# Moving all loads of a normalisation kernel to one DMA queue, with a 2 KB write ahead of the stores

## The chip, the cores and the metric

The kernel runs on one core of a Trainium2 chip. The metric is the device time of one execution in microseconds (us). Before the change it was 626.81 us, the median of 3 runs (626.70 to 626.87).

## The reference

Each of 4 x 8 x 16 = 512 channels of 256 x 256 float32 values is normalised to mean 0 and variance 1 and multiplied by its gamma:

```python
mu = x.mean(axis=(3, 4), keepdims=True)
var = ((x - mu) ** 2).mean(axis=(3, 4), keepdims=True)
out = (x - mu) / np.sqrt(var + 1e-5) * gamma[None, :, :, None, None]
```

134.2 MB are read and 134.2 MB are written, and each value takes few operations.

## The kernel before

The data is cut into 32 units of 128 rows x 8192 floats (4 MB; a row is 32 KB). Six slots in on-chip memory hold units. A unit is loaded, summed on VectorE (DVE), its squares are summed on ScalarE (ACT), a small matmul combines the rows of a channel, VectorE scales the slot in place, and the slot is stored. When the store has landed, the slot takes the load of the unit six further on. Loads are issued from SyncE's queue (SP), stores from ScalarE's. Only the first loads are dealt over both queues. The parts (`# ...` marks cuts):

```python
    def load(u, queue):
        queue.dma_start(out=slots[u % AHEAD][:], in_=xv[u])

    g_row = singles.tile([1, G * C], F32, name="g_row")
    for u in range(AHEAD):                       # AHEAD = 6
        if u == 1:
            nc.scalar.dma_start(out=g_row[:], in_=gv[None, :])
        load(u, nc.scalar if u in (1, 3) else nc.sync)
    # ...
    nc.vector.tensor_copy(out=g_rep[:], in_=g_row[:]...)          # gamma, before all units
    # ... 8 small matmuls spread gamma over the partitions
    nc.vector.tensor_copy(out=g_col[:], in_=g_ps[:])

    for u in range(U):                           # U = 32
        t = slots[u % AHEAD]
        nc.vector.reduce_sum(out=st[:, u, 0:1], in_=t[:], axis=AX.X)
        square = nc.scalar.activation(out=junk[:], in_=t[:], func=ACTF.Square, accum_out=st[:, u, 1:2])
        # ... matmul, variance, root, reciprocal, scale
        nc.vector.tensor_scalar(out=t[:], in0=t[:], scalar1=ps[:, 0:1],
                                scalar2=scale[:, u : u + 1], op0=ALU.add, op1=ALU.mult)
        nc.scalar.dma_start(out=ov[u], in_=t[:])
        if u + AHEAD < U:
            load(u + AHEAD, nc.sync)
```

## Time and profile before

| what | value | from |
|---|---|---|
| time, median of 3 | 626.81 us | runs |
| span in the profile | 625.2 us | page |
| DVE busy / ACT busy | 71% / 38% | page |
| share of the two DMA queues, of 16 engines' span | 52.8% + 46.8% | page |
| DMA rate | 429 GB/s mean, 436 in most slices | page |
| one 32 KB packet on one DMA engine | 1.213 us | packet records |
| 512 such packets one after another | 621.1 us (619.0 at the measured spacing) | product |
| from the start of one packet to the next on one engine | 1.209 us (the records overlap by 0.004) | packet records, median |

The next lines are from the profile page: the span, the mean busy share of the 16 DMA engines in 40 slices of 15.6 us (tenths), the GB/s moved in each slice, and the two queues with packets, MB and share of 16 engines' span. q1 is SyncE's queue, q10 ScalarE's.

```profile
span 625.2 us, 626 instructions
...
DMA  8999999999999999999999999999999999999998
GB/s 369 436 417 424 434 436 436 436 436 437 434 436 434 426 426 430 434 436 436 436 434 434 436 434 434 430 426 430 434 436 436 436 432 434 436 436 434 426 426 365
...
q10 hardware_dynamic: 4898, 142.61, 52.8%
q1 hardware_dynamic: 4320, 125.83, 46.8%
```

The two shares add to 99.6%: the DMA engines hardly ever rest. The slowest slices are the first and last, and the third and fourth, in which the first store begins; the others lie at 426 to 437.

The start of the timeline (start us, duration us, what; in brackets the idle time before it and what ended it):

```profile
0.80 1.90 SPq L48 DMA_DIRECT2D xt<-in_x_dram  x4
0.80 0.53 ACTq L54 DMA_DIRECT2D g_row<-in_gamma_dram  x1
...
1.37 0.84 ACTq L48 DMA_DIRECT2D xt<-in_x_dram  x2
...
2.06 0.68 DVE L79 COPY g_rep<-g_row 1x1024 f32<-1x1024 f32 x1 [2.06 <-DMA g_row<-in_gamma_dram]
...
20.32 8.69 DVE L103 TENSOR_REDUCE st<-xt 128x1 f32<-128x8192 f32 x1 [13.70 <-DMA xt<-in_x_dram]
...
35.38 0.35 ACTq L130 DMA_DIRECT2D out_dram<-xt  x1
```

gamma is there at 2.06 us, the first unit only at 20.32 (loads 0 and 1 share the engines), and the first store is issued at 35.38.

The waits view (who waited for what: us in total, times, longest), the time from issue to landing (KB each, median us), and the page's chain of work that ended last, by engine:

```profile
ACT junk L104 <- DMA xt<-in_x_dram: 229.0, 24, 16.6
DVE st L103 <- DMA xt<-in_x_dram: 111.2, 24, 13.7
```

```profile
out_dram<-xt ACTq DMA_DIRECT2D x32, 4096.0 KB, 67.1
xt<-in_x_dram SPq DMA_DIRECT2D x30, 4096.0 KB, 33.8
```

```profile
another core or an unknown queue 64%; DMA 16%; DVE 13%; SPq 1%; PE 1%; issue 0%; ACT 0%
```

Both compute engines wait for loads. A store takes 67 us to land though its own transfer is 8 packets on each engine, 9.7 us, so about seven such transfers (its own, other stores and the loads between them) pass meanwhile.

**Packet records.** The trace lists every DMA packet with start, duration, size and queue, but without its engine. I assigned each packet to the engine whose previous packet ended at that moment (within 12 ns). For the kernel before this gives 16 clean rows of 512 large packets. "Slow-packet time" below is the sum of what packets took above 1.213 us, divided by 16 engines. In the kernel before it is 0.71 us at the start, 0.62 us at about 43 us, where the first store's packets begin, and 0.08 us in all the time after 100 us.

### The profile page before, as it was taken

The page shows a single profiled execution, that of the slowest core. Times are in us where ns is not written, and L with a number is a line of the kernel's source. Part 1 is how long each engine was busy: PE and PEld are TensorE (multiplying, and loading weights), DVE is VectorE, ACT ScalarE, POOL GpSimd, SP SyncE. Part 2 cuts the span into 40 slices and gives each one's busy share as a digit, 9 for nine tenths or more (in the row PEclk, how much of TensorE's full clock was granted, in tenths as well). Part 3 has the DMA queues.
Part 4 walks back from the last instruction along what each step waited for, and adds up shares of the span by engine and source line. Part 5 has one row for each costly group of instructions (what it writes and reads, how often), then busy time and mean ns, then how long its engine had stood idle before and what let it go on. Part 6 is the DMA issues. An engine that isn't in the chain of part 4 may idle for free.

```text
span 625.2 us, 626 instructions
## 1 busy us (share of the span) xinstructions
PE 21.4 (3%) x80; PEld 19.5 (3%) x80; DVE 443.2 (71%) x162; ACT 238.8 (38%) x98; POOL 1.3 (0%) x9
## 2 busy tenths in 40 slices
PE   2000000000000000000000000000000000000000
PEld 2000000000000000000000000000000000000000
DVE  0699999998867668676687766776667867668620
ACT  0444444444444224443244432344423443224400
POOL 0000000000000000000000000000000000000000
DMA  8999999999999999999999999999999999999998
GB/s 369 436 417 424 434 436 436 436 436 437 434 436 434 426 426 430 434 436 436 436 434 434 436 434 434 430 426 430 434 436 436 436 432 434 436 436 434 426 426 365
DMA packets 9220, 268.46 MB, mean 429 GB/s; under 512 B 1025, under 2 KB 1026, under 8 KB 1026
## 3 DMA queue, kind: packets, MB, share of 16 engines
q10 hardware_dynamic: 4898, 142.61, 52.8%
q1 hardware_dynamic: 4320, 125.83, 46.8%
q14 instruction: 2, 0.02, 0.0%
HBM read 134.22 MB, written 134.22 MB: 429 GB/s over the span
## 4 chain that ended last, share of the span: by engine, by line
another core or an unknown queue 64%; DMA 16%; DVE 13%; SPq 1%; PE 1%; issue 0%; ACT 0%
DMA xt<-in_x_dram 9%; DVE st L103 8%; DMA out_dram<-xt 7%; DVE xt L126 4%; SPq L48 1%; PE ps L112 1%; ACT std L117 0%; DVE nvar L113 0%; DVE rstd L121 0%; DVE scale L123 0%
## 5 line engine op out<-in xcount | busy, mean ns | idle before, releaser
L103 DVE TENSOR_REDUCE st<-xt 128x1 f32<-128x8192 f32 x32 | 277.9, 8684 | 111.2 <-DMA xt<-in_x_dram 111.2
L104 ACT ACTIVATE junk<-xt 128x8192 uint8<-128x8192 f32 x32 | 225.0, 7030 | 272.2 <-DMA xt<-in_x_dram 229.0
L126 DVE TENSOR_SCALAR xt<-xt,ps,scale 128x8192 f32<-128x8192 f32 x32 | 145.6, 4550 | 1.2
L117 ACT ACTIVATE std<-nvar,eps_t 128x1 f32<-128x1 f32 x32 | 9.4, 294 | 79.6 <-DVE nvar L113 79.6
L112 PE MATMUL ps<-st,navg 128*128 128x2 f32 x64 | 17.9, 349 | 568.0 <-DVE st L103 568.0
L112 PEld LDWEIGHTS ps<-st,navg 128*128 128x128 f32 x64 | 16.0, 312 | 569.8 <-issue 569.8
L113 DVE TENSOR_SCALAR nvar<-ps 128x1 f32<-128x1 f32 x32 | 9.2, 287 | 23.8 <-PE ps L112 23.8
L121 DVE RECIPROCAL rstd<-std 128x1 f32<-128x1 f32 x32 | 5.3, 164 | 11.6 <-ACT std L117 11.6
L104 ACT ACTIVATION_READ_ACCUMULATOR junk<-xt 128x1 f32 x32 | 6.0, 186 | 0.0
L123 DVE TENSOR_TENSOR scale<-rstd,g_col 128x1 f32<-128x1 f32 x32 | 5.1, 159 | 1.1
L84 PE MATMUL g_ps<-one,g_rep 1*128 1x1 f32 x16 | 3.5, 346 | 2.9 <-DVE g_rep L79 2.9
L84 PEld LDWEIGHTS g_ps<-one,g_rep 1*128 1x128 f32 x16 | 3.5, 325 | 2.9 <-POOL navg L68 2.9
L90 DVE COPY g_col<-g_ps 128x8 f32<-128x8 f32 x1 | 0.2, 166 | 3.7 <-PE g_ps L84 3.7
L74 ACT ACT_TABLE_LOAD x1 | 1.3, 1283 | 2.2 <-issue 2.2
L79 DVE COPY g_rep<-g_row 1x1024 f32<-1x1024 f32 x1 | 0.7, 681 | 2.1 <-DMA g_row<-in_gamma_dram 2.1
L64 POOL TENSOR_SCALAR_AFFINE_SELECT navg<-navg 128x128 f32<-128x128 f32 x1 | 0.4, 403 | 0.1
L68 POOL TENSOR_SCALAR_AFFINE_SELECT navg<-navg 128x128 f32<-128x128 f32 x1 | 0.4, 398 | 0.1
L63 POOL MEMSET navg<- 128x128 f32 x1 | 0.2, 220 | 0.0
L74 ACT ACTIVATE root_eps<-eps_t 128x1 f32<-128x1 f32 x1 | 0.2, 203 | 0.0
L147 POOL MEMSET const-bfloat16-1.0<- 128x1 bf16 x1 | 0.1, 101 | 0.0
L147 POOL MEMSET const-uint8-127<- 128x1 uint8 x1 | 0.1, 101 | 0.0
L147 POOL MEMSET const-float32-0.0<- 128x1 f32 x1 | 0.1, 98 | 0.3 <-issue 0.3
(3 smaller groups left out, 0.3 us busy)
## 6 DMA issues: line engine op xcount, KB each, us to landing
out_dram<-xt ACTq DMA_DIRECT2D x32, 4096.0 KB, 67.1
xt<-in_x_dram SPq DMA_DIRECT2D x30, 4096.0 KB, 33.8
xt<-in_x_dram ACTq DMA_DIRECT2D x2, 4096.0 KB, 33.3
g_row<-in_gamma_dram ACTq DMA_DIRECT2D x1, 0.5 KB
```

The source lines that it names most:

```text
L48: queue.dma_start(out=slots[u % AHEAD][:], in_=xv[u])
L74: nc.scalar.activation(out=root_eps[:], in_=eps_t[:], func=ACTF.Sqrt)
L79: nc.vector.tensor_copy(out=g_rep[:], in_=g_row[:].rearrange("o (n k) -> o n k", n=NG).unsqueeze(3).to_broadcast([1, NG, K, S]),)
L84: nc.tensor.matmul(out=g_ps[:, n : n + 1], lhsT=g_rep[:, n].rearrange("o k s -> o (k s)"), rhs=one[:], start=True, stop=True,)
L103: nc.vector.reduce_sum(out=st[:, u, 0:1], in_=t[:], axis=AX.X)
L104: square = nc.scalar.activation(out=junk[:], in_=t[:], func=ACTF.Square, accum_out=st[:, u, 1:2],)
L112: nc.tensor.matmul(out=ps[:], lhsT=navg_w, rhs=st[:, u], start=True, stop=True)
L113: nc.vector.tensor_scalar(out=nvar[:, u : u + 1], in0=ps[:, 0:1], scalar1=ps[:, 0:1], scalar2=ps[:, 1:2], op0=ALU.mult, op1=ALU.add,)
L117: nc.scalar.activation(out=std[:, u : u + 1], in_=nvar[:, u : u + 1], func=ACTF.Sqrt, bias=eps_t[:], scale=-1.0,)
L121: nc.vector.reciprocal(out=rstd[:, u : u + 1], in_=std[:, u : u + 1])
L123: nc.vector.tensor_mul(out=scale[:, u : u + 1], in0=rstd[:, u : u + 1], in1=g_col[:, g : g + 1],)
L126: nc.vector.tensor_scalar(out=t[:], in0=t[:], scalar1=ps[:, 0:1], scalar2=scale[:, u : u + 1], op0=ALU.add, op1=ALU.mult,)
```

## The change

The intent can only be inferred: the loads become one plain stream, and a tiny early write to `out` may pay in advance what the first store pays. 32 rows of the first output unit get 64 bytes each, two rows per DMA engine, which the real store overwrites later.

```diff
-    def load(u, queue):
-        queue.dma_start(out=slots[u % AHEAD][:], in_=xv[u])
-
+    def load(u):
+        nc.sync.dma_start(out=slots[u % AHEAD][:], in_=xv[u])
 
     g_row = singles.tile([1, G * C], F32, name="g_row")
+
+    touch = singles.tile([P, 16], F32, name="touch")
+    nc.vector.memset(touch[:], 0.0)
     for u in range(AHEAD):
-        if u == 1:
+        load(u)
+        if u == 0:
+            nc.scalar.dma_start(out=ov[0, 0::4, 0:16], in_=touch[0::4])
             nc.scalar.dma_start(out=g_row[:], in_=gv[None, :])
-        load(u, nc.scalar if u in (1, 3) else nc.sync)
 ...
-            load(u + AHEAD, nc.sync)
+            load(u + AHEAD)
```

## The prediction

> **What bounds the kernel now.** The DMA engines, nearly without a pause. The page's third part puts the queues at 52.8% and 46.8% of 16 engines' span, 99.6% together; its second part shows about 436 GB/s in most slices and 429 on average. DVE is busy 71%, ACT 38%. In the trace's DMA packet records every one of the 8192 packets of 32 KB takes about 1.213 us, 512 follow each other on each of 16 engines, and hardly any gap is over 0.1 us: 512 x 1.213 = 621.1 us of a 625.2 us span. (The Trainium skill, "DMA: Bandwidth & Descriptors", section "Where 436 GB/s comes from", gives a ceiling of 435 GB/s; 16 x 32,768 B / 1.213 us = 432 agrees.) So only about 4 us is not pure transfer:
> - about 2.1 us before the first load packet moves, though the first load is issued at 0.80 (timeline);
> - the engines' first packet, 2.0 us instead of 1.2: about 0.9 us with its successors;
> - one bubble at 41 to 44 us, where ScalarE's queue turns from its last load to the first store: 22 packets take 1.3 to 1.9 us, together about 0.65 us per engine;
> - about 1.3 us after the last store packet.
>
> The waits view's long times (ACT for loads 229 us, DVE 111 us) are engines waiting for this traffic.
>
> **What the change does.**
> 1. Loads 1 and 3 move from ScalarE's queue to SP's. Bytes and packets stay. The same skill page, "Issuing engines are not separate DMA queues", says that both queues feed the same engines, so no bandwidth is lost or won; in this trace packets from one queue alone (the last 20 us, stores only) also take 1.213 us. Load 0 no longer shares with load 1: it lands near 11.9 us (estimate: 8 packets x 1.21 + 2.1) instead of 20.3, the first reduction starts there, and the first store is issued near 27 us instead of 35.4. That moves compute by 8 us, all hidden: six loads are 58 us of transfer, and the queues stay non-empty until the end.
> 2. The touch: 2048 bytes, 32 rows of 64 B, two per engine, behind a tiny DVE memset. Its presumable aim is to pay each engine's first-write cost during startup. If the 0.65 us bubble is a first-write cost, up to 0.65 us is saved; if it comes from a queue turning from loads to stores, part 1 already removes it, since ScalarE's queue then holds no large loads. The touch itself may add 0.1 to 0.5 us at the start (estimate: two tiny packets per engine, and the same bubble in the worst case).
>
> **On the critical path:** only the bubble and the start, under 1 us of 627. I expect about 0.4 us less.
>
> **Predicted: 626.4 us, range 625.6 to 627.3.** Chances: faster by over 2% 0.01, within 2% 0.98, slower by over 2% 0.01.
>
> **What would show it.** Steps 1: the first DVE reduction starts near 12 us, the first store's issue is near 27 us, queue bytes 134 MB on each, DMA rate 436 in the middle slices. Step 2: no packets over 1.3 us at the first store; slightly longer first packets. Wrong: the same bubble at about 28 us; a first slice clearly below 369 GB/s.
>
> **What would make it wrong.** A single queue with six loads could leave gaps between packets (slices under 430 before 28 us). The small writes to rows 128 KB apart could stall the engines for microseconds at the start. Another phase between loads and stores could change the packet time itself.

## The result, and the profile after

The changed kernel took 627.20 us (median of 4 runs, 627.09 to 627.40), before 626.84 us beside it (4 runs, 626.70 to 627.08). The ratio is 1.0006 with a 95% interval of 0.9988 to 1.0023: the same. (Ratios here are the mean time of one kernel's fast runs over that of the other's in the same rounds, so not quite the ratio of the quoted medians.) Executions over 1.5% slower than the fastest of the same kernel are left out of the means.

The page, for the lines shown of before:

```profile
span 625.4 us, 628 instructions
...
DMA  9999999999999999999999999999999999999998
GB/s 369 436 413 428 434 436 436 436 436 436 434 436 432 428 424 432 434 436 434 436 436 436 434 436 434 425 428 434 430 436 434 436 436 436 434 434 436 428 432 354
...
q1 hardware_dynamic: 4608, 134.22, 49.9%
q10 hardware_dynamic: 4658, 134.22, 49.7%
```

The two shares are 99.6% again; the bytes are now even. The first slice has the same 369 GB/s, so one queue feeds the engines as well as two did. The third slice has its dip again (413, it was 417).

The timeline:

```profile
0.98 0.58 ACTq L57 DMA_DIRECT2D out_dram<-touch  x1
...
1.60 0.67 ACTq L58 DMA_DIRECT2D g_row<-in_gamma_dram  x1
...
11.74 0.68 DVE L82 COPY g_rep<-g_row 1x1024 f32<-1x1024 f32 x1 [10.80 <-DMA g_row<-in_gamma_dram]
...
13.11 7.03 ACT L107 ACTIVATE junk<-xt 128x8192 uint8<-128x8192 f32 x1 [9.30 <-DMA xt<-in_x_dram]
16.15 0.17 DVE L93 COPY g_col<-g_ps 128x8 f32<-128x8 f32 x1 [3.73 <-PE g_ps L87]
16.23 8.67 DVE L106 TENSOR_REDUCE st<-xt 128x1 f32<-128x8192 f32 x1
...
31.28 0.39 ACTq L133 DMA_DIRECT2D out_dram<-xt  x1
```

Load 0 is there at 13.1 us, when ACT starts on it, 7 us earlier than before. But DVE starts only at 16.23. In DVE's program order the two copies for gamma stand before the first reduction, and gamma now arrives at 11.7 us instead of 2.06, because it is issued behind the touch on ScalarE's queue. In the packet records the touch's two 64-byte packets per engine start near 6.1 and 7.3 us, its completion packet near 8.6, gamma's 512 bytes at 10.1: one small packet per 1.2 us, each taking turns with a 32 KB load packet. The Trainium skill, "DMA: Bandwidth & Descriptors", section "Queues, rings and completion order", says that an engine goes round its queues packet by packet; this trace agrees from 6.1 us on, and shows what that costs a small transfer. The turns are not the whole delay: the touch was issued at 0.98 us, and three load packets pass on every engine before its first packet. In the kernel before, load 1 (issued at 1.37, first packet at 6.13) waits as long, and the first stores of the kernels with all loads on SyncE's queue start 3.5 to 4.9 us after their issue. The turn-taking alone does not explain this, and no run here does.

Waits, landing times and chain:

```profile
ACT junk L107 <- DMA xt<-in_x_dram: 251.2, 27, 10.1
DVE st L106 <- DMA xt<-in_x_dram: 111.2, 26, 5.1
```

```profile
xt<-in_x_dram SPq DMA_DIRECT2D x32, 4096.0 KB, 53.2
out_dram<-xt ACTq DMA_DIRECT2D x32, 4096.0 KB, 47.8
out_dram<-touch ACTq DMA_DIRECT2D x1, 2.0 KB, 8.5
```

```profile
DVE 71%; another core or an unknown queue 18%; PE 4%; DMA 2%; ACT 2%; issue 1%; ACTq 0%
```

Three things are to be seen. DVE waits for loads for exactly as long as before, 111.2 us. The landing times moved from 67.1 + 33.8 = 100.9 us to 47.8 + 53.2 = 101.0 us: the waiting went from the store queue to the load queue and its sum stayed, as it must when six slots circulate at an unchanged rate. And the chain view turned from "unknown queue 64%, DVE 13%" to "DVE 71%" while the time stayed: it follows one of several equally tight chains, and which one it picks says little here (run `dve_pad` tests this).

The slow-packet time at the first store is still there: 0.65 us per engine at about 34 us, 16 packets of 1.65 to 2.03 us, one before each engine's first store packet. The touch did not remove it.

### The profile page after: what moved, and what is told of

Its sections match the earlier page's. It is cut to its first block, busy times and chain, and to the rows that moved or that the text cites. A ratio compares the mean times of both kernels' runs of the same rounds, so it can differ in the third digit from the quotient of the medians.

```text
span 625.4 us, 628 instructions
## 1 busy us (share of the span) xinstructions
PE 21.4 (3%) x80; PEld 19.6 (3%) x80; DVE 443.5 (71%) x163; ACT 238.8 (38%) x98; POOL 1.3 (0%) x9
## 4 chain that ended last, share of the span: by engine, by line
DVE 71%; another core or an unknown queue 18%; PE 4%; DMA 2%; ACT 2%; issue 1%; ACTq 0%
DVE st L106 44%; DVE xt L129 23%; PE ps L115 3%; DMA g_row<-in_gamma_dram 2%; ACT std L120 2%; DVE nvar L116 2%; DVE rstd L124 1%; DVE scale L126 1%; PE g_ps L87 1%; DVE g_rep L82 0%; ACTq L57 0%; DVE g_col L93 0%; DVE touch L53 0%
## 5 line engine op out<-in xcount | busy, mean ns | idle before, releaser
L106 DVE TENSOR_REDUCE st<-xt 128x1 f32<-128x8192 f32 x32 | 277.9, 8684 | 111.2 <-DMA xt<-in_x_dram 111.2
## 6 DMA issues: line engine op xcount, KB each, us to landing
xt<-in_x_dram SPq DMA_DIRECT2D x32, 4096.0 KB, 53.2
out_dram<-xt ACTq DMA_DIRECT2D x32, 4096.0 KB, 47.8
```

## The experiments

The theory after the result: the DMA engines are always full, so neither part of the change matters. Rivals: the touch, or the load order, costs the 0.36 us between the medians; or early compute is exposed after all.

### `sp_only`: the loads on SP, no touch

```diff
-    touch = singles.tile([P, 16], F32, name="touch")
-    nc.vector.memset(touch[:], 0.0)
-            nc.scalar.dma_start(out=ov[0, 0::4, 0:16], in_=touch[0::4])
```

> All loads on SP's queue, no touch, gamma first on ScalarE's queue. Theory (the 16 DMA engines are full all the time, so neither part matters): within 0.3 us of before (626.8). Rival 1 (the touch costs the 0.36 us between the two medians): 626.8 or less. Rival 2 (the load order costs it): 627.2. All: the gamma row lands near 2 us, the first DVE reduction starts near 13 us and the first store is issued near 28 us. The slow packet before the first store stays, about 1.8 us on each engine, if it belongs to the first large store and not to what ScalarE's queue did before.

Measured: 627.78 us (5 runs, 627.36 to 629.15) beside 626.91 (9 runs). The ratio 1.0018 has an interval of 1.0005 to 1.0031, so it is a little slower than before. The theory's 0.3 us is missed; so is rival 1, as the only cost. The first store was issued at 28.00 us, and the slow-packet time at it was 1.12 us per engine.

### `touch_only`: the touch, with loads 1 and 3 on ScalarE's queue as before

```diff
+    touch = singles.tile([P, 16], F32, name="touch")
+    nc.vector.memset(touch[:], 0.0)
         if u == 1:
+            nc.scalar.dma_start(out=ov[0, 0::4, 0:16], in_=touch[0::4])
             nc.scalar.dma_start(out=g_row[:], in_=gv[None, :])
```

> Loads 1 and 3 stay on ScalarE's queue; the touch and then gamma are issued there in front of them. Theory: within 0.3 us of before. Rival 1 (the touch costs 0.36 us): near 627.2. Rival 2 (load order): 626.8. Gamma lands late (near 10 us), because small transfers take turns with 32 KB load packets; load 0 lands near 20 us as before.

Measured: 627.34 us (5 runs), ratio 1.0007 (0.9993 to 1.0021): the same as before and as the changed kernel. By the medians it is 0.43 us over before (626.91), more than the theory's 0.3 and near rival 1's 627.2; its five runs (627.24 to 627.38) all lie above the nine of before (626.67 to 627.13). So a cost of the touch of about 0.4 us is neither shown nor excluded. gamma landed late as expected (DVE's copy at 11.4 us). Load 0 landed at 16.7 us, not 20: the touch and gamma also delayed the two loads behind them on that queue.

### `gamma_first`: the changed kernel with gamma ahead of the touch

```diff
-            nc.scalar.dma_start(out=ov[0, 0::4, 0:16], in_=touch[0::4])
             nc.scalar.dma_start(out=g_row[:], in_=gv[None, :])
+            nc.scalar.dma_start(out=ov[0, 0::4, 0:16], in_=touch[0::4])
```

> As the changed kernel, but gamma goes ahead of the touch. Gamma should land near 2 to 7 us instead of 11.7, the first DVE reduction should start near 13 us instead of 16.2 and every early store 3 us earlier. Theory: no change of the total (627.0 +- 0.3), because that 3 us lies in DVE's slack. Rival (early compute is exposed): about 3 us less.

Its timeline:

```profile
2.05 0.68 DVE L82 COPY g_rep<-g_row 1x1024 f32<-1x1024 f32 x1 [1.10 <-DMA g_row<-in_gamma_dram]
...
13.01 8.69 DVE L106 TENSOR_REDUCE st<-xt 128x1 f32<-128x8192 f32 x1 [6.39 <-DMA xt<-in_x_dram]
...
28.07 0.38 ACTq L133 DMA_DIRECT2D out_dram<-xt  x1
```

Compute and the first store came 3.2 us earlier, as expected, and the time was 628.24 us (5 runs, 627.37 to 628.44; ratio to before 1.0018, 1.0005 to 1.0031). The rival that early compute is exposed (3 us less) falls. But it was not the same either: it lost about 1 us, like `sp_only`, which shares with it the early gamma, the first reduction at 13 us and the first store at 28.0 us, but not the touch. That suggested a new theory: **the moment at which the first store meets the stream of loads matters.**

### `dve_pad`: 73 us more work on DVE

(Here and below, the line that allocates the tile `pad` is left out.)

```diff
+        nc.vector.reduce_sum(out=pad[:, u : u + 1], in_=t[:, 0:2048], axis=AX.X)
         nc.scalar.dma_start(out=ov[u], in_=t[:])
```

> The changed kernel with one more DVE reduction (128x2048, an estimated 2.2 us, a quarter of the 8.68 us one) in each of 32 units, about 70 us more DVE work. The changed kernel's chain view puts 71% of the span on DVE. Theory (DMA bound, the chain is one of several equal ones): total within 0.5 us of 627.2, DVE wait for loads falls from 111 us to about 40 us. Rival (DVE bound, as the chain says): near 627 + 70 = 697 us, or at least 640.

The 32 added reductions took 2.29 us each, 73.2 us in all. The wait and the chain:

```profile
DVE st L107 <- DMA xt<-in_x_dram: 44.5, 21, 3.1
```

```profile
DVE 82%; another core or an unknown queue 7%; PE 3%; DMA 2%; ACT 2%; issue 2%; ACTq 0%
```

DVE's wait for loads fell from 111.2 to 44.5 us, and 628.75 us (4 runs, 627.87 to 630.48) is nowhere near 697: DVE is not the limit, whatever its share of the chain. Still the rise of 1.55 us over the changed kernel is more than the 0.5 us expected. In the profiled execution the engines ended at 623.4 us on average (after: 623.2), and one alone at 627.2.

### `big_touch`: the early write as one whole 32 KB row per engine

```diff
-    touch = singles.tile([P, 16], F32, name="touch")
-    nc.vector.memset(touch[:], 0.0)
+    nc.vector.memset(slots[5][:], 0.0)
-            nc.scalar.dma_start(out=ov[0, 0::4, 0:16], in_=touch[0::4])
+            nc.scalar.dma_start(out=ov[0, 0::8], in_=slots[5][0::8])
```

> As the changed kernel, but the touch is 16 whole rows of 32 KB (one large packet per engine, 0.5 MB in all), taken from the sixth slot after a DVE memset. If the slow packet at the first store is paid once, by the first large write of each engine, it moves to this early write (one packet near 1.8 us on each engine before 25 us) and is gone at the first real store; total = after + about 1.2 us (one more packet per engine). If it is paid whenever stores start while loads run, it shows at both places; total = after + about 1.8 us.

Measured: fast runs 628.58 to 628.86 us (a fourth, 641.11, was slow). That is about 1.6 us over the changed kernel, 1.2 of it one more packet per engine. The slow packets moved to the early write (0.71 us per engine before 25 us) and were gone at the first real store (0.01). Nothing is won: the cost is paid earlier, and the extra packet comes on top.

### `reload`: units 16 to 21 loaded twice, so that the store queue runs dry

```diff
             load(u + AHEAD)
+            if 16 <= u + AHEAD < 22:
+                load(u + AHEAD)
```

> As the changed kernel, but units 16 to 21 are loaded twice into their slots, the second load waiting for the first. The store queue runs dry there and stores start again beside loads. If the slow packet is a cost of the first large write only, no load packet beside a restarted store exceeds 1.3 us; if it is a cost of each start of stores, about 0.6 us per engine shows at each restart. Total: 6 x 9.7 us more traffic and waits, 690 to 750 us; not meant to be fast.

Measured: 695.85 us (one run, its state unknown). Slow packets came back wherever stores started again beside loads: 0.77, 0.33, 0.55 and 0.54 us per engine near 317, 347, 377 and 407 us. They also came where loads started again (0.66, 0.55, 0.34 and 0.31 us near 303, 334, 363 and 393 us). So this is not a cost of an engine's first write alone. It does not fit `big_touch`, where stores started a second time without it. What exactly causes these 0.65 us stays open.

### `sp_late3` and `sp_late10`: only the first store moved

Both are `sp_only` with one or two more reductions on DVE in front of the first unit alone.

```diff
         t = slots[u % AHEAD]
+        if u == 0:
+            nc.vector.reduce_sum(out=pad[:, 0 : 1], in_=t[:, 0:3104], axis=AX.X)     # sp_late3
+            # sp_late10: two, of 8192 and of 944 columns
```

> The kernel with all loads on SP and no touch (which lost about 0.9 us to before and whose first store was issued at 28.0 us), with one more DVE reduction of 3104 columns (estimate 3.3 us) in front of the first unit's, so that the first store is issued near 31.3 us as in the changed kernel. Theory (what matters is the moment at which the first stores meet the loads, not the touch): about 0.65 us of slow packets per engine at the first store as in the changed kernel, total near 627.2. Rival (the touch itself, or gamma's place, makes the changed kernel quicker than the one without it): stays near 627.8 with about 1.1 us of slow packets.

> The same, with two more reductions (8192 and 944 columns, estimate 9.7 us, the time of one load), so that the first store is issued near 37.7 us, again at the same place within a load as at 28.0. If the loss belongs to that place (the first store packets beside the first packets of a new load), the slow packets are again about 1.1 us per engine and the total near 627.8; if it belongs to an early first store as such, about 0.6 us and near 627.0, though compute starts 10 us later. If late compute itself cost time, it would be slower than 627.8.

Measured, beside 627.16 us of before: `sp_late3`, first store issued at 31.43 us, 627.00 us (5 runs, ratio 0.9997); `sp_late10`, first store at 37.83 us, 627.59 us (5 runs, ratio 1.0007, 0.9995 to 1.0020). Delaying the first compute by 3.4 us gave back what `sp_only` had lost, without a touch. But the slow-packet time at the first store was 0.87 us per engine, not the 0.65 expected; the changed kernel, with the touch and its first store at nearly the same time, had 0.65. Delaying it by 9.8 us gave back less: slow packets at the first store 0.84 us per engine, and 0.30 after it. Both fit the theory of the moment, though 627.59 alone would not carry it.

### `big_touch_far` and `touch_4k`: other early writes

The first writes the same 16 whole rows into the last unit of `out`, the second only 4 KB of each of the 16 rows.

```diff
-            nc.scalar.dma_start(out=ov[0, 0::8], in_=slots[5][0::8])
+            nc.scalar.dma_start(out=ov[U - 1, 0::8], in_=slots[5][0::8])                   # big_touch_far
+            nc.scalar.dma_start(out=ov[0, 0::8, 0:1024], in_=slots[5][0::8, 0:1024])       # touch_4k (and a shorter memset)
```

> As the early write of 16 whole rows, but into the last unit of out instead of the first. There the slow packets moved to the early write (0.71 us per engine) and were gone at the first real store (0.0). Theory 1 (a cost of the first large write of each engine, wherever it goes): the same again, none at the first real store near 43 us. Theory 2 (a cost of the first large write to an address range): about 0.6 us per engine at both places.

> As the early write of 16 whole rows, but only the first 4 KB of each (64 KB in all). If any write well above 64 bytes pays the start cost ahead, the slow packets at the first real store are gone (under 0.1 us per engine), and the total is near 627; if it takes whole large packets, about 0.6 us per engine stays at the first real store.

`big_touch_far` behaved as `big_touch` (fast runs 628.58 to 628.90 us; slow packets 0.81 us at the early write, 0.00 at the first store; one run of 638.64 was slow). So the address written does not matter.

`touch_4k` was a surprise: fast runs 642.97 to 645.41 us (one of 667.90 was slow), ratio 1.0274. A write of 64 KB in all cannot cost 17 us as traffic (the whole kernel moves 268 MB in 625). Its first slow packets were no worse than usual (0.85 us), but 10.1 us per engine of slow packets were spread over all the time after 100 us. Its first store was issued at 30.27 us.

### `touch_4k_late` and `sp_late2`: is it the 4 KB write or the moment?

`touch_4k_late` adds a reduction of 1056 columns in front of `touch_4k`'s first unit. `sp_late2` is `sp_late3` with 1848 columns instead of 3104; it has no early write at all.

```diff
         t = slots[u % AHEAD]
+        if u == 0:
+            nc.vector.reduce_sum(out=pad[:, 0 : 1], in_=t[:, 0:1056], axis=AX.X)     # sp_late2: 0:1848
```

> The kernel with the 4 KB early writes, which took 645 us and whose first store was issued at 30.27 us, with one more DVE reduction of 1056 columns (estimate 1.3 us) in front of the first unit's, so that the first store is issued near 31.5 us. In the 645 us run 13 engines had 26 packets of loads before their first store packet and 3 had 27; in before and after all 16 agree. Theory (the moment of the first store decides whether the engines stay in step, and being out of step costs the time): all or 15 engines agree, total near 627. Rival (the early 4 KB write itself slows the engines): stays over 640.

> The kernel with all loads on SP and no touch, with a reduction of 1848 columns (estimate 2.1 us) in front of the first unit's, so that the first store is issued near 30.1 us, at about the same place within a load packet as in the 645 us run. Theory (moment of the first store): the engines split between 26 and 27 load packets, total clearly above 627.8, up to 645. Rival (the 4 KB write itself): 627 to 628, as at 28.0 and 31.4 us.

Measured, beside 627.02 us of before (`touch_4k` and `sp_late3` above ran beside 627.16): `touch_4k_late` 627.47 us (4 runs, 627.40 to 627.48); `sp_late2` 644.24 us (4 runs, 643.28 to 646.12; ratio 1.0279, 1.0258 to 1.0300). The slices and the first store of each pair, the slow kernel first. `sp_late2`:

```profile
GB/s 379 436 410 439 424 424 424 439 420 422 421 422 426 432 413 430 412 434 432 412 428 412 434 428 410 426 420 428 426 420 420 412 430 416 424 428 410 436 359 286
```

```profile
30.09 0.38 ACTq L133 DMA_DIRECT2D out_dram<-xt  x1
```

`sp_late3`, which differs from it in the length of the added reduction alone:

```profile
GB/s 369 436 402 436 436 436 436 436 434 434 428 432 434 428 432 434 436 434 436 436 434 434 432 432 428 436 430 432 436 436 434 436 434 434 434 428 432 434 430 365
```

```profile
31.43 0.38 ACTq L133 DMA_DIRECT2D out_dram<-xt  x1
```

`touch_4k`:

```profile
GB/s 366 450 399 431 423 429 438 421 423 431 426 429 425 417 432 409 435 431 415 427 415 431 431 413 435 409 433 417 425 431 405 438 415 425 435 419 421 431 382 280
```

```profile
30.27 0.39 ACTq L132 DMA_DIRECT2D out_dram<-xt  x1
```

`touch_4k_late`:

```profile
GB/s 373 436 402 436 436 436 436 436 436 434 429 429 432 427 430 436 436 434 436 436 434 436 436 432 432 425 432 432 434 436 434 436 436 436 434 436 432 429 427 358
```

```profile
31.26 0.39 ACTq L135 DMA_DIRECT2D out_dram<-xt  x1
```

Adding about 1 us of idle work to the slow kernel made it 17 us faster (fast runs, 644.7 to 627.5), and taking 1.3 us away from the delay in the quick kernel (`sp_late3`, first store at 31.43) made it 17 us slower, with no early write involved. The whole course of the run, not its start, differs: between the first three and the last two slices, 405 to 439 GB/s in the slow kernels against 425 to 436 in the quick ones. The moment of the first store (with the first unit's compute, which the added reduction moves too) decides, and the 4 KB write does not. All four runs of `sp_late2` were slow and none of `sp_late3` and `touch_4k_late`, so chance is not the reason. The reverse was not tested: the single slow runs of `big_touch` (641.11) and `big_touch_far` (638.64) lost 10 to 12 us against their fast runs, have no profile, and may be the same effect.

One detail of the expectation fell. I had thought that the engines must *disagree* about how many load packets go before their first store packet. In `sp_late2` all 16 agree, on 26. Counting that number in each run gives:

| run | first store issued, us | load packets before an engine's first store packet (engines) | that number modulo 8 | time, us |
|---|---|---|---|---|
| before | 35.38 | 35 (16) | 3 | 626.8 |
| touch_only | 31.73 | 38 (15), 40 (1) | 6, 0 | 627.3 |
| changed kernel | 31.28 | 27 (16) | 3 | 627.2 |
| touch_4k_late | 31.26 | 27 (16) | 3 | 627.5 |
| sp_late3 | 31.43 | 27 (15), 28 (1) | 3, 4 | 627.0 |
| dve_pad | 30.96 | 27 (15), 26 (1) | 3, 2 | 628.8 |
| sp_late10 | 37.83 | 33 (9), 32 (7) | 1, 0 | 627.6 |
| sp_only | 28.00 | 24 (10), 25 (6) | 0, 1 | 627.8 |
| gamma_first | 28.07 | 24 (10), 25 (6) | 0, 1 | 628.2 |
| touch_4k | 30.27 | 26 (13), 27 (3) | 2, 3 | 644.7 |
| sp_late2 | 30.09 | 26 (16) | 2 | 644.2 |

(The times are medians of the fast runs, against before's 626.8 to 627.2. A load or store is 8 packets per engine, so the number modulo 8 says how far into a load the first store begins. In `before` and `touch_only` the first store also queues behind load 3 on ScalarE's queue, so it comes later after its issue.) Once the queues take turns, this offset is kept: in the changed kernel the order of packets at the start, load L and store S, is `SLSLSLSLSLSSLSLLSLSLSL`, and in `sp_late2` it is `SLSLSLSLSLSLSSLLSLSLSL`, and either goes on in this way. (`reload` starts like the changed kernel; `big_touch` and `big_touch_far`, where a large early store packet goes first, have 32 on 14 or 15 engines and hardly any slow packets after it, 0.1 us per engine.)

With an offset of 3 on all engines, or on 15 with 4 on one (`sp_late3`), and with 6 on 15 engines (`touch_only`), the runs are at full speed. With 0 and 1 mixed they lose up to about 1 us, nearly all of it near the beginning. With 2 on 13 or 16 engines they lose 17 us, spread over the run.

`dve_pad` allows a comparison inside one execution: the one engine with 26 had 2.6 us of slow packets between 38 and 550 us, the other 15 at most 0.7. It is also the straggler at 627.2 us. The records carry no engine numbers, but the order of packets marks it: up to 537 us only its row has the order `SSLL` of `sp_late2`, where the others have `SSLSLL`; then that row and another exchange orders (they count 509 and 515 packets instead of 512), and the row that now has `SSLL` ends at 627.2. The offset of one engine is not all, though: in `touch_4k` the three engines with 27 were slowed between 38 and 100 us as much as the others (0.64 to 1.34 us against 0.21 to 1.28).

Shown: the moment of the first store and first compute decides between 627 and 644 us. Correlated only, in two kernels and in one engine of a third: that it does so through the offset of 2. Open: why that order of packets makes the engines slow. In `sp_late2` most of the early slow packets are loads that stand second in a pair `LL`, up to 0.35 us each at first, and later the engines drift apart; no run here says what happens inside the engine.

## Why the prediction was right or wrong

- **The time: right.** 627.20 us lies in 625.6 to 627.3, though only 0.1 us from its upper end, and "within 2%" holds. ("Only about 4 us is not pure transfer" is nearer to 6: packets follow each other every 1.209 us, so 512 take 619.0 of 625.2.) The ground was right too: 99.6% of 16 engines' span are used before and after. `dve_pad` (73 us more DVE work, 1.55 us more time) and `gamma_first` (3.2 us earlier start, nothing gained) show that compute is hidden.
- **The direction: not seen.** "I expect about 0.4 us less" became 0.36 us more at the medians, with an interval that holds 1. No claim is made for either sign.
- **Moving the loads: right on bandwidth.** The first slice has 369 GB/s in both, and the spacing of packets is the same from one queue. This is what the Trainium skill, "DMA: Bandwidth & Descriptors", section "Issuing engines are not separate DMA queues", led one to expect.
- **The step that failed first: "the first reduction starts there [near 11.9 us], and the first store is issued near 27 us".** Measured: 16.23 and 31.28 us. Load 0 was used from 13.1 us on: the estimate had left out the 0.7 us of slow first packets and the landing time. The larger part is gamma: behind the touch it waits for three load packets and then needs five turns with 32 KB packets, and arrives at 11.7 us, and two DVE copies that depend on it stand before the first reduction.
- **The touch: the hoped-for term is zero.** "Up to 0.65 us is saved" measured 0.62 us of slow-packet time before and 0.65 after; the sign named in advance, "the same bubble", came, at 34 us instead of 28. Of "0.1 to 0.5 us at the start" the slow packets show nothing (0.71 before, 0.72 after); in the total it stays open (`touch_only` is 0.43 us over before at the medians, within the interval). `big_touch` shows that a whole large packet per engine does move the bubble, at 1.2 us for that packet. The other guess, that moving the loads alone would remove it, is refuted by `sp_only`, with 1.12 us.
- **The risk: named, but much too lightly.** "Another phase between loads and stores could change the packet time itself" was right as a possibility. The changed kernel stays at full speed with its first store at 31.28 us; kernels that differ from it only at the start ran 2.7% slower with it at 30.09 and 30.27. A chance of 0.01 for slower was too small for a change that moves the first store by microseconds; that it landed on a good place was not foreseen. What the touch really did was to delay gamma and with it the first store, from 28.0 us in `sp_only` to 31.3.

None of the 12 versions beats the kernel before by a margin that the rounds can resolve; `sp_late3` equals it (ratio 0.9997, 0.9984 to 1.0009).

## What to carry to other kernels

If two DMA queues together fill the engines for the whole run, reordering the start cannot win more than the gaps that the packets show (here 1 to 2 us of 627), so count those first. But it can lose: in this kernel the offset between the two steady streams was set when the second one started and was kept to the end, so when a harmless edit costs some per cent evenly over the run, shift the first store by a microsecond or two before you blame the edit. Put small transfers that something waits for ahead of the large ones, since each of their packets takes a turn with a large one.

## What the Trainium skill lacked or had wrong

- "DMA: Bandwidth & Descriptors", section "Issuing engines are not separate DMA queues", names only the issue time as what the choice of queue changes, and has nothing on the moment at which a second stream starts. Here a shift of the first store by 1.3 us on ScalarE's queue, against loads on SyncE's, changed the steady rate of the rest of the run: 627.0 against 644.2 us (`sp_late3`, `sp_late2`).
- The same page, section "Queues, rings and completion order", has the turn-taking by packets, and the traces agree, but not its cost for small transfers: gamma's 512 bytes arrived at 11.7 us behind the touch and at 2.06 us ahead of the large loads. Nor has it the wait before the first turn: three load packets, until 6.1 us, for a touch issued at 0.98 us.
- No page that I read has the slow packets at the first large store beside running loads, 0.62 to 1.12 us per engine here, which a 64-byte or a 4 KB early write does not remove and a 32 KB one moves (`big_touch`, 0.71 us at the early write).
- The ceiling of 435 GB/s in the same page's section "Where 436 GB/s comes from" agrees: 32,768 B x 16 / 1.213 us = 432 GB/s in the packets, 436 in most slices. The section's lower limit of about 358 GB/s for transfers between HBM and on-chip memory did not bind this one-core run, which moved 429 GB/s on average.
